# First feed-forward product of a decoder layer: two of eight pairs of k-tiles as seven block products instead of eight

## The chip, the cores and the metric

The kernel runs on one core of a Trainium2 chip. The metric is the device time of one execution in microseconds. Three executions of the kernel before took 1478.36, 1482.99 and 1483.57 us (median 1482.99); the profiled execution took 1481.03 us, of which its trace spans 1478.9 us.

## The reference

One layer of a decoder over 256 tokens of width 2048: a token mixer, a cross attention and a gated feed-forward part, each followed by a residual and a LayerNorm. Only the feed-forward part is touched:

```python
def swiglu(x, w_in, w_out):          # x 256x2048, w_in 2048x11264, w_out 5632x2048
    g, u = jnp.split(x @ w_in, 2, axis=-1)
    return (jax.nn.silu(g) * u) @ w_out
```

The left half of the columns of `x @ w_in` is the gate, the right half the linear part.

## The kernel before

Every float32 product is made of three TensorE passes. `split` (lines 116 to 118) writes a high part (ScalarE, `ACTIVATE`, L117) and a low part (VectorE, source minus high part, `TENSOR_TENSOR`, L118) of an operand; the product is then high x high, high x low, low x high, accumulated in PSUM (L229 to L231 in `chunk_mm`, or L268 to L270 in `mm3`).

The activations x (`x2T`, four `Quad`s of 4 k-tiles x 256 tokens) lie transposed and split in SBUF. The weights are streamed. `chunk_in` (L199) loads a chunk of two k-tiles x 512 columns (512 KB) into one of 5 `raw` buffers and splits it into one of 4 `hl` buffers; `chunk_mm` then runs 6 matmuls for each of the two token tiles, so a chunk is 12 matmuls of 128x512. `product` (L233) does this for 8 chunks.

The first feed-forward product has 11 column groups `j` of 512 columns (here: rounds). A round is a `product` for the gate columns, whose two PSUM tiles go through Silu (L865, ScalarE), and a `product` for the linear columns; VectorE then multiplies the two (L877), and `keep` writes the result h to DRAM (L196, a 256 KB `spill` in two DMAs). To be the stationary operand of the second feed-forward product, h must be transposed: `turned` loads it back from DRAM in another order (four DMAs, L181, tile `turn`), transposes it in blocks on VectorE (four instructions, L187, tile `tr`), and splits it (ScalarE L188, VectorE L190). `turn` is a generator; `flush` advances it by one step after each chunk of the next product: loads after its first chunk, transposes and L188 after the second, L190 after the third.

All loads, spills and turns are issued by SyncE's one queue (SP), in order. A load waits until the chunk five before it has been split (`raw` has 5 buffers); the split of a chunk waits until TensorE has used the chunk four before it (`hl` has 4). The written order is only a start: a scheduler that simulates a timeline reorders the instructions of each engine, and that order is then fixed. [...] The pool `big` holds 14 tiles `b8` of 8 KB per partition, a `Quad` in each.

Of the kernel before, what the change touches and what calls it, by code (L numbers as in the profile page):

```python
# [28 lines left out]
DFF = 5632  # L29
# [36 lines left out]
def trunk(ctx: ExitStack, tc: tile.TileContext, a, out: bass.AP):  # L66
    nc = tc.nc
    const = ctx.enter_context(tc.tile_pool(name="const", bufs=1))
    big = ctx.enter_context(tc.tile_pool(name="big", bufs=14))
    stream = ctx.enter_context(tc.tile_pool(name="stream", bufs=3))  # L70
    work = ctx.enter_context(tc.tile_pool(name="work", bufs=2))
# [60 lines left out]
    for tt in range(NT):  # L132
        k = P * (tt + 1)
# [88 lines left out]
    def chunk_mm(o, act, tt, c, kts, n, w):  # L222
        hi, lo = w
        sl = slice(tt * P, (tt + 1) * P)
        for kk in range(KC):
            k = c * KC + kk
            q = act[k // 4]
            xh, xl = q.hi[:, k % 4, sl], q.lo[:, k % 4, sl]
            nc.tensor.matmul(o[:, :n], xh, hi[:, kk, :n], start=k == 0, stop=False)  # L229
            nc.tensor.matmul(o[:, :n], xh, lo[:, kk, :n], start=False, stop=False)  # L230
            nc.tensor.matmul(o[:, :n], xl, hi[:, kk, :n], start=False, stop=k == kts - 1)  # L231

    def product(act, pieces, steps=1, before=None, first=None, seq=0, stream_seq=0, done=None):  # L233
# [137 lines left out]
    for ps in wide(w_in[:, C_QI:C_KI], load_x):  # L371
        t = b8().rearrange("p (h t) -> p h t", h=8)
        for tt in range(NT):
            sl = slice(tt * P, (tt + 1) * P)
# [3 lines left out]
            for i in range(2):  # L378
                p = ps_aux(F32R)
# [19 lines left out]
    for tt in range(NT):  # L399
        sl = slice(tt * P, (tt + 1) * P)  # L400
        p = ps[tt]
# [6 lines left out]
        st = work.tile([P, 6], F32, tag="st1", name=nm("st1"))  # L408
# [260 lines left out]
    for j in range(4):  # L669
        cs = slice(j * W, (j + 1) * W)  # L670
# [5 lines left out]
    for j in range(4):  # L676
        cs = slice(j * W, (j + 1) * W)
# [3 lines left out]
        for tt in range(NT):  # L681
            g = stage()
# [18 lines left out]
    tok = []  # L701
# [101 lines left out]
    for j in range(4):  # L803
        cs = slice(j * W, (j + 1) * W)
# [28 lines left out]
    ws = {}  # L833
# [21 lines left out]
    x2T = n2.quads  # L855


    hT = []
    wf = a["w_ffn_in"][0]
    for j in range(DFF // W):  # L860
        gs = []

        def gate(tt, p):
            g = stage()
            nc.scalar.activation(g, p, AF.Silu)  # L865
            gs.append(g)

        if j == 0:
# [5 lines left out]
        q = Quad()  # L874
        d = spill()
        for tt in range(NT):
            nc.vector.tensor_tensor(gs[tt], gs[tt], pu[tt], op=ALU.mult)  # L877
            keep(d, tt, gs[tt])
# [36 lines left out]
```

## Time and profile before

| | |
|---|---|
| times of 3 runs | 1478.36, 1482.99, 1483.57 us |
| profiled execution, its span | 1481.03, 1478.9 us |
| TensorE (PE) busy | 1456.7 us, 98% |
| VectorE (DVE) busy | 917.5 us, 62% |
| ScalarE (ACT) busy | 670.8 us, 45% |
| GpSimd (POOL) busy | 19.5 us, 1% |
| DMA queue, share of 16 engines | 69.4% |
| loads of the first feed-forward weights | 176 of 512 KB |

Matmuls are pipelined, so that a record of one is longer than the step to the next, and busy TensorE says only that there was always one under way. The 176 loads are 11 rounds of 16 chunks.

### The profile page before, as it was taken

What the parts mean: (1) busy time and instruction counts of PE and PEld (TensorE: products, weight loads), DVE (VectorE), ACT (ScalarE), POOL (GpSimd) and SP (SyncE); (2) the same over time, 40 slices, a digit from 0 to 9 for tenths busy, and PEclk for the clock granted to TensorE, in tenths of its full rate; (3) what the DMA queues carried; (4) which work ended last, traced back from release to release, by engine and by line L of the source; (5) the groups of instructions that cost most, each with busy time, mean ns of one, the idle gap of its engine ahead of it and who ended that gap; (6) DMA issues with size and microseconds to landing.
All of it is one profiled execution on the core that took longest, in us unless ns stands there. A gap on an engine that the chain in (4) does not pass through costs nothing.

```text
span 1478.9 us, 17743 instructions
## 1 busy us (share of the span) xinstructions
PE 1456.7 (98%) x6656; PEld 1210.6 (82%) x6656; DVE 917.5 (62%) x1151; ACT 670.8 (45%) x778; POOL 19.5 (1%) x43
## 2 busy tenths in 40 slices
PE   8999999999999999999989999999999999999997
PEld 6988888888888888888778888888888888888885
DVE  5575986575856666885875455555545555545446
ACT  4554456454544444545544344444444444343331
POOL 0000000000000000000000000000000000000000
PEclk9999999999999999999999999999999999999998
DMA  9884667777667779968536766676667667666662
GB/s 281 189 272 143 197 216 225 230 237 222 221 191 233 219 259 305 229 191 264 171 129 201 226 215 212 219 223 222 206 207 233 213 216 254 190 197 196 193 220 100
DMA packets 197462, 316.60 MB, mean 214 GB/s; under 512 B 18688, under 2 KB 58752, under 8 KB 197376
## 3 DMA queue, kind: packets, MB, share of 16 engines
q1 hardware_dynamic: 197376, 315.47, 69.4%
q8 instruction: 52, 0.85, 0.3%
q14 instruction: 34, 0.28, 0.1%
HBM read 298.65 MB, written 16.78 MB: 213 GB/s over the span
## 4 chain that ended last, share of the span: by engine, by line
PE 93%; DMA 3%; DVE 2%; issue 1%; POOL 0%; ACT 0%; SPq 0%; POOLq 0%; DVEq 0%; ACTq 0%
PE acc L230 29%; PE acc L231 29%; PE acc L229 29%; DMA raw<-in_w_in 1%; PE aux L269 1%; PE aux L270 1%; PE aux L268 1%; DVE b L751 1%; DMA turn<-spill 1%; DMA kvg<-in_kv_norm_g 1%; PE acc L269 0%; PE acc L270 0%; DVE hl L118 0%; DVE lnst L733 0%; PE acc L268 0%
## 5 line engine op out<-in xcount | busy, mean ns | idle before, releaser
L118 DVE TENSOR_TENSOR hl<-raw,hl 128x1024 fp32r<-128x1024 f32 (+2 forms) x495 | 596.2, 1212 | 432.1 <-ACT hl L117 431.4
L117 ACT ACTIVATE hl<-raw 128x1024 fp32r<-128x1024 f32 (+2 forms) x495 | 517.7, 1052 | 604.5 <-PE acc L231 541.5
L230 PE MATMUL acc<-hl,b 128*128 128x512 f32 (+1 forms) x1912 | 743.1, 389 | 0.3 <-DVE hl L118 0.2
L231 PE MATMUL acc<-hl,b 128*128 128x512 f32 (+1 forms) x1912 | 742.9, 389 | 0.0
L229 PE MATMUL acc<-hl,b 128*128 128x512 f32 (+1 forms) x1912 | 740.9, 389 | 0.7 <-ACT b L117 0.7
L230 PEld LDWEIGHTS acc<-hl,b 128*128 128x128 f32 x1912 | 359.4, 188 | 73.4 <-DVE hl L118 1.1
L229 PEld LDWEIGHTS acc<-hl,b 128*128 128x128 f32 x1912 | 359.4, 188 | 73.2 <-ACT b L117 0.9
L231 PEld LDWEIGHTS acc<-hl,b 128*128 128x128 f32 x1912 | 359.4, 188 | 73.1 <-DVE b L118 0.2
L187 DVE STREAM_TRANSPOSE tr<-turn 128x256 f32<-128x256 f32 (+1 forms) x148 | 67.0, 510 | 82.5 <-DMA turn<-spill 82.5
L188 ACT ACTIVATE b<-tr 128x1024 fp32r<-128x1024 f32 (+1 forms) x37 | 37.4, 1014 | 92.4 <-DVE tr L187 89.1
L190 DVE TENSOR_TENSOR b<-tr,b 128x1024 fp32r<-128x1024 f32 (+1 forms) x37 | 42.8, 1162 | 3.5 <-ACT b L188 3.0
L117 ACT ACTIVATE b<-aux 128x512 fp32r<-128x512 f32 (+1 forms) x48 | 25.6, 542 | 37.3 <-PE aux L161 21.6
L118 DVE TENSOR_TENSOR b<-aux,b 128x512 fp32r<-128x512 f32 (+1 forms) x48 | 28.7, 617 | 3.8 <-ACT b L117 3.6
L230 PE MATMUL acc<-b,b 128*128 128x512 f32 x72 | 28.2, 394 | 1.3 <-DVE b L118 1.3
L229 PE MATMUL acc<-b,b 128*128 128x512 f32 x72 | 28.1, 394 | 0.1
L231 PE MATMUL acc<-b,b 128*128 128x512 f32 x72 | 27.9, 390 | 0.0
L269 PE MATMUL acc<-hl,b 128*128 128x512 f32 x64 | 25.4, 404 | 0.5 <-DVE hl L118 0.4
L270 PE MATMUL acc<-hl,b 128*128 128x512 f32 x64 | 24.6, 394 | 0.0
L118 DVE TENSOR_TENSOR b<-raw,b 128x1024 fp32r<-128x1024 f32 x18 | 21.4, 1218 | 5.0 <-ACT b L117 5.0
L269 PE MATMUL aux<-b,b 128*128 128x256 f32 (+1 forms) x80 | 21.8, 281 | 0.0
L268 PE MATMUL acc<-hl,b 128*128 128x512 f32 x64 | 20.7, 410 | 1.1 <-ACT hl L117 1.1
L865 ACT ACTIVATE stage<-acc 128x512 f32<-128x512 f32 x22 | 13.2, 599 | 18.7 <-PE acc L231 18.7
(123 smaller groups left out, 569.9 us busy)
## 6 DMA issues: line engine op xcount, KB each, us to landing
raw<-in_w_ffn_in SPq DMA_DIRECT2D x176, 512.0 KB, 4.2
raw<-in_w_in SPq DMA_DIRECT2D x143, 512.0 KB, 4.4
raw<-in_w_ffn_out SPq DMA_DIRECT2D x88, 512.0 KB, 4.3
raw<-in_w_out SPq DMA_DIRECT2D x32, 512.0 KB, 8.0
spill<-stage SPq DMA_DIRECT2D x56, 256.0 KB, 4.0
turn<-spill SPq DMA_DIRECT2D x104, 128.0 KB, 3.3
raw<-in_w_o_dsa SPq DMA_DIRECT2D x16, 512.0 KB, 4.7
raw<-in_w_o_moba SPq DMA_DIRECT2D x16, 512.0 KB, 4.4
```

The source lines that it names most:

```text
L117: nc.scalar.activation(hi, src, AF.Copy)
L118: return (eng or nc.vector).tensor_tensor(lo, src, f(hi), op=ALU.subtract)
L187: nc.vector.transpose(tr[:, i, :], v[:, i])
L188: nc.scalar.activation(hi, tr, AF.Copy)
L190: nc.vector.tensor_tensor(lo, tr, f(hi), op=ALU.subtract)
L229: nc.tensor.matmul(o[:, :n], xh, hi[:, kk, :n], start=k == 0, stop=False)
L230: nc.tensor.matmul(o[:, :n], xh, lo[:, kk, :n], start=False, stop=False)
L231: nc.tensor.matmul(o[:, :n], xl, hi[:, kk, :n], start=False, stop=k == kts - 1)
L268: nc.tensor.matmul(o, lh, rh, start=start, stop=False)
L269: nc.tensor.matmul(o, lh, rl, start=False, stop=False)
L270: nc.tensor.matmul(o, ll, rh, start=False, stop=stop)
L751: prev = nc.vector.scalar_tensor_tensor(t, t, scalar, self.rows[row][:, j * W:(j + 1) * W], op0=op0, op1=op1)
```

## The change

Round 0 stays as it was. Rounds 1 to 10 do the gate and the linear columns together. For a pair of k-tiles (chunk `c`), the two token tiles x two k-tiles are a 2x2 block matrix A, and two k-tiles x (gate, linear) are a 2x2 block matrix B; the result is a 2x2 block of PSUM tiles (x11, x12, x21, x22). `plain_cell` makes the eight block products of a chunk as before (two chunks, 24 matmuls). `fast_cell`, for the chunks 0 and 1 only (fast cells A and B here), makes seven products in the Strassen-Winograd form: 21 matmuls. For that it needs

- on the activation side, four sums per chunk, made once in round 0 (`fast_acts`: 8 additions of 128x128, 8 transposes, split into the `Quad` `sq`);
- on the weight side, in every round, four subtractions of 128x512 on VectorE (`tb`, `tcs`) and four splits, of the 1024-wide B11/B12 (`ha`), `tb` (`hb`), `tcs` (`hc`) and of the 512-wide B22;
- on the output side, four more PSUM banks for the products m1, m5, m6, m7, taken from `aux`, and `sums` (one copy, four additions, VectorE), whose results are added to x11 to x22 at the round's end.

The round's end is now six VectorE instructions (L990, L992, L993) in place of two (L877). The chunks run in the order 0, 2, 3, 1, 4, 5, 6, 7.

```diff
+    FAST = (0, 1)
+    ORDER = (0, 2, 3, 1, 4, 5, 6, 7)
...
+    def fast_acts():
+        q = Quad()
+        for t, c in enumerate(FAST):
+            st = stage()
...
+            nc.vector.tensor_tensor(s1, a21, a22, op=ALU.add)
+            nc.vector.tensor_tensor(s2, s1, a11, op=ALU.subtract)
+            nc.vector.tensor_tensor(s3, a11, a21, op=ALU.subtract)
+            nc.vector.tensor_tensor(s4, a12, s2, op=ALU.subtract)
+            to_quad(q, t, st)
+        return q
...
+            self.t[name] = ps_acc() if name[0] == "x" else ps_aux()
...
+    def fast_cell(bk, act, sq, t, c, ws, stop):
...
+        r0, r1 = [load_chunk(w, c) for w in ws]
+        ha, la = hl_tile()
+        lows.append(split(ha, la, r0))
+        hb, lb = hl_tile()
+        tb = work.tile([P, 2, W], F32, tag="tw", name=nm("tw"), bufs=1)
+        nc.vector.tensor_tensor(tb[:, 0], r1[:, 0], r0[:, 0], op=ALU.subtract)
+        nc.vector.tensor_tensor(tb[:, 1], r1[:, 1], r1[:, 0], op=ALU.subtract)
+        hc, lc = hl_tile()
+        tcs = work.tile([P, 2, W], F32, tag="s", name=nm("s"))
+        nc.vector.tensor_tensor(tcs[:, 0], r1[:, 1], tb[:, 0], op=ALU.subtract)
+        nc.vector.tensor_tensor(tcs[:, 1], r0[:, 1], tcs[:, 0], op=ALU.subtract)
+        b22 = work.tile([P, 2, W], F32R, tag="s", name=nm("s"))
+        split(b22[:, 0], b22[:, 1], r1[:, 1])
+        split(hb, lb, tb)
+        lows.append(split(hc, lc, tcs))
+        bk.mm("m1", a11, (ha[:, 0], la[:, 0]), stop)
+        bk.mm("m5", s1, (hb[:, 0], lb[:, 0]), stop)
+        bk.mm("m7", s3, (hb[:, 1], lb[:, 1]), stop)
+        bk.mm("m6", s2, (hc[:, 0], lc[:, 0]), stop)
+        bk.mm("x11", a12, (ha[:, 1], la[:, 1]))
+        bk.mm("x12", s4, (b22[:, 0], b22[:, 1]))
+        bk.mm("x21", a22, (hc[:, 1], lc[:, 1]))
...
+    def plain_cell(bk, act, c, ws, stop):
...
+            for tt in range(NT):
+                for kk in range(KC):
+                    bk.mm(f"x{tt + 1}{n + 1}", act_of(q, k + kk, tt), (hi[:, kk], lo[:, kk]), stop and kk == KC - 1)
+            flush()
...
+    def sums(bk):
+        m = bk.t
+        c11, c12, c21, c22 = [stage() for _ in range(4)]
+        nc.scalar.activation(c11, m["m1"], AF.Copy)
+        nc.vector.tensor_tensor(c12, c11, m["m6"], op=ALU.add)
+        nc.vector.tensor_tensor(c21, c12, m["m7"], op=ALU.add)
+        nc.vector.tensor_tensor(c12, c12, m["m5"], op=ALU.add)
+        nc.vector.tensor_tensor(c22, c21, m["m5"], op=ALU.add)
...
-            product(x2T, [wf[:, j * W:(j + 1) * W]], done=gate)
-        pu = product(x2T, [wf[:, DFF + j * W:DFF + (j + 1) * W]])
...
+            for i, c in enumerate(ORDER):
+                if c in FAST:
+                    fast_cell(bk, x2T, sq, FAST.index(c), c, ws, c == FAST[-1])
+                    flush()
...
+                    if c == FAST[-1]:
+                        cs = sums(bk)
+                else:
+                    plain_cell(bk, x2T, c, ws, i == len(ORDER) - 1)
+            for tt in range(NT):
+                g, u = cs[2 * tt:2 * tt + 2]
+                nc.vector.tensor_tensor(g, g, bk.t[f"x{tt + 1}1"], op=ALU.add)
+                nc.scalar.activation(g, g, AF.Silu)
+                nc.vector.tensor_tensor(u, u, bk.t[f"x{tt + 1}2"], op=ALU.add)
+                nc.vector.tensor_tensor(g, g, u, op=ALU.mult)
+                keep(d, tt, g)
```

The scheduler's order on three places of a middle round. First VectorE, where the transposes of the last round's h stand. Before, just after the multiplication of a round and three splits of the next:

```order
L877 TENSOR_TENSOR stage_1107_7491<-stage_1107_7491,acc_1109_7495 128x512
L877 TENSOR_TENSOR stage_1108_7493<-stage_1108_7493,acc_1110_7496 128x512
L118 TENSOR_TENSOR hl_1140_7706<-raw_1139_7704,hl_1140_7706 128x1024
L118 TENSOR_TENSOR hl_1142_7723<-raw_1141_7721,hl_1142_7723 128x1024
L118 TENSOR_TENSOR hl_1144_7740<-raw_1143_7738,hl_1144_7740 128x1024
L187 STREAM_TRANSPOSE tr_1136_7680<-turn_1133_7658 128x256 x4
L118 TENSOR_TENSOR hl_1146_7757<-raw_1145_7755,hl_1146_7757 128x1024
L190 TENSOR_TENSOR b8_1127_7633<-tr_1136_7680,b8_1127_7633 128x1024
```

Now they stand amid the work for fast cell B (`raw_1106`, `raw_1107` are its two chunks, `tw` is `tb`, `s_1112` `tcs`, `s_1113` B22, and `hl_1108`, `hl_1109`, `hl_1111` are `ha`, `hb`, `hc`):

```order
L915 TENSOR_TENSOR tw_1110_7275<-raw_1107_7269 128x512
L187 STREAM_TRANSPOSE tr_1098_7208<-turn_1095_7186 128x256 x4
L918 TENSOR_TENSOR s_1112_7279<-raw_1107_7269,tw_1110_7275 128x512
L118 TENSOR_TENSOR hl_1108_7271<-raw_1106_7267,hl_1108_7271 128x1024
L118 TENSOR_TENSOR s_1113_7282<-raw_1107_7269,s_1113_7282 128x512
L919 TENSOR_TENSOR s_1112_7279<-raw_1106_7267,s_1112_7279 128x512
L190 TENSOR_TENSOR b8_1022_6803<-tr_1098_7208,b8_1022_6803 128x1024
L118 TENSOR_TENSOR hl_1109_7274<-tw_1110_7275,hl_1109_7274 128x1024
L118 TENSOR_TENSOR hl_1111_7278<-s_1112_7279,hl_1111_7278 128x1024
L118 TENSOR_TENSOR hl_1119_7321<-raw_1118_7319,hl_1119_7321 128x1024
```

Between the transposes and the split of the next plain chunk (`hl_1119`, chunk 4) stand seven instructions, where there was none. In the rounds 8 and 9 L190 is not there: those `Quad`s find no free `b8` until round 10. In round 10 L187 stands behind `hc`.

Second VectorE at the end of a round. Before, the plain splits run up to the multiplication (the rows are of another round, its last three chunks):

```order
L118 TENSOR_TENSOR hl_1174_7941<-raw_1173_7939,hl_1174_7941 128x1024
L118 TENSOR_TENSOR hl_1177_7963<-raw_1176_7961,hl_1177_7963 128x1024
L118 TENSOR_TENSOR hl_1180_7986<-raw_1179_7984,hl_1180_7986 128x1024
L877 TENSOR_TENSOR stage_1149_7789<-stage_1149_7789,acc_1151_7793 128x512
```

Now fast cell A of the next round (chunks `raw_1136`, `raw_1137`) is prepared ahead of the round's end; `hl_1129`, `hl_1131`, `hl_1133` are the plain chunks before it. The load of `raw_1137` waits for the buffer of `raw_1126`, which the split of `hl_1127` frees:

```order
L118 TENSOR_TENSOR hl_1127_7389<-raw_1126_7387,hl_1127_7389 128x1024
L118 TENSOR_TENSOR hl_1129_7406<-raw_1128_7404,hl_1129_7406 128x1024
L914 TENSOR_TENSOR tw_1140_7475<-raw_1137_7469,raw_1136_7467 128x512
L915 TENSOR_TENSOR tw_1140_7475<-raw_1137_7469 128x512
L118 TENSOR_TENSOR hl_1131_7423<-raw_1130_7421,hl_1131_7423 128x1024
L918 TENSOR_TENSOR s_1142_7479<-raw_1137_7469,tw_1140_7475 128x512
L118 TENSOR_TENSOR s_1143_7482<-raw_1137_7469,s_1143_7482 128x512
L919 TENSOR_TENSOR s_1142_7479<-raw_1136_7467,s_1142_7479 128x512
L118 TENSOR_TENSOR hl_1133_7440<-raw_1132_7438,hl_1133_7440 128x1024
```

Two 512-wide subtractions that need both chunks of cell A now stand ahead of the split of `hl_1131`; behind `hl_1133` come `ha`, `hb`, two L990, `hc`, two L992 and two L993.

Third TensorE. Before, a chunk's 12 matmuls stand in written order, high, low, high, as here its first three:

```order
L229 MATMUL acc_1129_7639<-hl_1144_7740,b8_903_6017 128x512
L230 MATMUL acc_1129_7639<-hl_1144_7740,b8_903_6017 128x512
L231 MATMUL acc_1129_7639<-hl_1144_7740,b8_903_6017 128x512
```

In fast cell B the matmuls that need only a high part are drawn ahead; its last ten:

```order
L268 MATMUL aux_1091_7170<-hl_1111_7278,b8_943_6305 128x512
L268 MATMUL acc_1094_7182<-hl_1111_7278,b8_901_6015 128x512
L269 MATMUL aux_1089_7162<-hl_1109_7274,b8_943_6305 128x512
L270 MATMUL aux_1089_7162<-hl_1109_7274,b8_943_6305 128x512
L269 MATMUL aux_1090_7166<-hl_1109_7274,b8_943_6305 128x512
L270 MATMUL aux_1090_7166<-hl_1109_7274,b8_943_6305 128x512
L269 MATMUL aux_1091_7170<-hl_1111_7278,b8_943_6305 128x512
L270 MATMUL aux_1091_7170<-hl_1111_7278,b8_943_6305 128x512
L269 MATMUL acc_1094_7182<-hl_1111_7278,b8_901_6015 128x512
L270 MATMUL acc_1094_7182<-hl_1111_7278,b8_901_6015 128x512
```

The low part of `hc` is first read by the fourth matmul from the cell's end, the eighteenth of 21.

## Rows read from the trace of the kernel before

**Rows 1.** The page: busy time, and the chain that ended last.

```profile
PE 1456.7 (98%) x6656; PEld 1210.6 (82%) x6656; DVE 917.5 (62%) x1151; ACT 670.8 (45%) x778; POOL 19.5 (1%) x43
PE 93%; DMA 3%; DVE 2%; issue 1%; POOL 0%; ACT 0%; SPq 0%; POOLq 0%; DVEq 0%; ACTq 0%
```

**Rows 2.** Windows: us, busy by engine, granted clock, DMA; ten rounds, sum and mean.

```profile
985.00:1028.00 43.00, 43.00 (x192) 35.61 (x191) 22.68 (x23) 18.38 (x20) 0.00 (x0) 1.00 0.68 215
...
sum 435.00, PE 435.00 PEld 360.32 DVE 233.46 ACT 183.67 POOL 0.00; mean PE 43.50 PEld 36.03 DVE 23.35 ACT 18.37 POOL 0.00
```

**Rows 3.** Timeline of PE: start, us; two matmuls twelve apart in one product.

```profile
1000.30 0.39 PE L229 MATMUL acc<-hl,b 128*128 128x512 f32 x1
...
1003.02 0.39 PE L229 MATMUL acc<-hl,b 128*128 128x512 f32 x1
```

**Rows 4.** Timeline of DVE around a round's end; brackets: idle before, and releaser.

```profile
1009.75 1.23 DVE L118 TENSOR_TENSOR hl<-raw,hl 128x1024 fp32r<-128x1024 f32 x1 [1.50 <-ACT hl L117]
1010.89 1.28 DVE L877 TENSOR_TENSOR stage<-stage,acc 128x512 f32<-128x512 f32 x2
...
1022.50 2.17 DVE L187 STREAM_TRANSPOSE tr<-turn 128x256 f32<-128x256 f32 x4 [3.36 <-DMA turn<-spill]
1024.60 1.18 DVE L118 TENSOR_TENSOR hl<-raw,hl 128x1024 fp32r<-128x1024 f32 x1
```

**Rows 5.** Timeline of DVE, an earlier product: a chain of 512-wide instructions.

```profile
452.84 1.28 DVE L693 TENSOR_TENSOR stage<-stage,acc 128x512 f32<-128x512 f32 x2
454.04 1.28 DVE L694 TENSOR_TENSOR stage<-stage,b 128x512 f32<-128x512 f32 x2
455.24 1.22 DVE L118 TENSOR_TENSOR hl<-raw,hl 128x1024 fp32r<-128x1024 f32 x1
```

**Rows 6.** Timeline of SP around the same round's end as in the DVE rows.

```profile
1011.60 0.94 SPq L196 DMA_DIRECT2D spill<-stage  x2
1013.73 0.38 SPq L210 DMA_DIRECT2D raw<-in_w_ffn_in  x1
1016.63 1.80 SPq L181 DMA_DIRECT2D turn<-spill  x4
```

**Rows 7.** Waits, ten rounds: engine line waited for, us in total, times, longest.

```profile
DVE hl L118 <- ACT hl L117: 161.0, 121, 2.0
DVE tr L187 <- DMA turn<-spill: 30.9, 10, 5.0
```

**Rows 8.** Timeline of DVE: the longest and the shortest way from L877 to L187.

```profile
1097.93 1.28 DVE L877 TENSOR_TENSOR stage<-stage,acc 128x512 f32<-128x512 f32 x2
1111.17 2.17 DVE L187 STREAM_TRANSPOSE tr<-turn 128x256 f32<-128x256 f32 x4 [4.99 <-DMA turn<-spill]
...
1141.45 1.28 DVE L877 TENSOR_TENSOR stage<-stage,acc 128x512 f32<-128x512 f32 x2
1151.80 2.20 DVE L187 STREAM_TRANSPOSE tr<-turn 128x256 f32<-128x256 f32 x4 [2.11 <-DMA turn<-spill]
```

**Rows 9.** Tile `raw`, ten rounds: the last line, on its loads.

```profile
DMA to landing us min/median/max: 3.4/4.2/7.4
```

**Rows 10.** Lines: groups of instructions, busy us, mean ns of one, idle before.

```profile
L117 ACT ACTIVATE hl<-raw 128x1024 fp32r<-128x1024 f32 (+2 forms) x495 | 517.7, 1052 | 604.5 <-PE acc L231 541.5 <-DMA raw<-in_w_in 18.5 <-issue 16.6
L230 PEld LDWEIGHTS acc<-hl,b 128*128 128x128 f32 x1912 | 359.4, 188 | 73.4 <-DVE hl L118 1.1
...
L694 DVE TENSOR_TENSOR stage<-stage,b 128x512 f32<-128x512 f32 x8 | 5.1, 683 | 0.0
```

**Rows 11.** Tile `stage`: ns min/median/max, first and last start; eight transposes.

```profile
L161 PE MATMUL aux<-ident,stage x8: 270/272/273, 689.4 to 690.7; 128*128 128x128 f32 x8
```

More of the change, by code (lines that the diff above doesn't have):

```diff
@@ L855, in trunk @@
     x2T = n2.quads
+    FAST = (0, 1)
[4 more added lines that the diff above has]
+            st = stage()
+            a11, a12 = [tok[0][:, (2 * c + i) * P:(2 * c + i + 1) * P] for i in range(2)]
+            a21, a22 = [tok[1][:, (2 * c + i) * P:(2 * c + i + 1) * P] for i in range(2)]
+            s1, s2, s3, s4 = [st[:, i * P:(i + 1) * P] for i in range(4)]
+            nc.vector.tensor_tensor(s1, a21, a22, op=ALU.add)
[4 more added lines that the diff above has]
+        return q
@@ new lines, in trunk, with __init__, mm, load_chunk @@
+    class Banks:
+        def __init__(self, last_cell):
+            self.t, self.begun = {}, set()
+            self.last_cell = last_cell
+        def mm(self, name, x, w, stop=False):
+            if name not in self.t:
+                self.t[name] = ps_acc() if name[0] == "x" else ps_aux()
+            (xh, xl), (wh, wl) = x, w
+            mm3(self.t[name], xh, xl, wh, wl, name not in self.begun, stop)
+            self.begun.add(name)
+    def load_chunk(w, c, mixed=False):
+        raw = stream.tile([P, KC, W], F32, tag="raw", name=nm("raw"), bufs=5)
+        last[0] = nc.sync.dma_start(raw, w[c * KC * P:(c + 1) * KC * P, :].rearrange("(k p) n -> p k n", p=P))
+        return raw
@@ new lines, in hl_tile, with act_of @@
+    def hl_tile():
+        t = stream.tile([P, D], F32R, tag="hl", name=nm("hl"), bufs=4)
+        return [t[:, i * KC * W:(i + 1) * KC * W].rearrange("p (k n) -> p k n", k=KC) for i in range(2)]
+    def act_of(q, k, tt):
+        sl = slice(tt * P, (tt + 1) * P)
+        return q.hi[:, k, sl], q.lo[:, k, sl]
+    def fast_cell(bk, act, sq, t, c, ws, stop):
+        q, k = act[c * KC // 4], c * KC % 4
+        a11, a12, a22 = act_of(q, k, 0), act_of(q, k + 1, 0), act_of(q, k + 1, 1)
+        s1, s2, s3, s4 = [act_of(sq, i, t) for i in range(4)]
+        r0, r1 = [load_chunk(w, c) for w in ws]
[20 more added lines that the diff above has]
+        bk.mm("x21", a22, (hc[:, 1], lc[:, 1]))
@@ new lines, in plain_cell @@
+    def plain_cell(bk, act, c, ws, stop):
+        q, k = act[c * KC // 4], c * KC % 4
+        for n, w in enumerate(ws):
+            raw = load_chunk(w, c)
+            hi, lo = hl_tile()
+            lows.append(split(hi, lo, raw))
+            for tt in range(NT):
+                for kk in range(KC):
+                    bk.mm(f"x{tt + 1}{n + 1}", act_of(q, k + kk, tt), (hi[:, kk], lo[:, kk]), stop and kk == KC - 1)
+            flush()
+            side.step(1)
+    def sums(bk):
[6 more added lines that the diff above has]
+        nc.vector.tensor_tensor(c22, c21, m["m5"], op=ALU.add)
+        return c11, c12, c21, c22
@@ L858, in trunk @@
     hT = []
     wf = a["w_ffn_in"][0]
+    sq = None
     for j in range(DFF // W):
@@ L866, in gate @@
             gs.append(g)
+        q = Quad()
+        d = spill()
         if j == 0:
@@ L870, in trunk @@
             side.finish()
-        else:
-            product(x2T, [wf[:, j * W:(j + 1) * W]], done=gate)
-        pu = product(x2T, [wf[:, DFF + j * W:DFF + (j + 1) * W]])
[L874 to L878, printed above, removed]
+            sq = fast_acts()
+            pu = product(x2T, [wf[:, DFF + j * W:DFF + (j + 1) * W]])
+            for tt in range(NT):
+                nc.vector.tensor_tensor(gs[tt], gs[tt], pu[tt], op=ALU.mult)
+                keep(d, tt, gs[tt])
+        else:
+            ws = [wf[:, j * W:(j + 1) * W], wf[:, DFF + j * W:DFF + (j + 1) * W]]
+            bk = Banks(None)
+            for i, c in enumerate(ORDER):
+                if c in FAST:
+                    fast_cell(bk, x2T, sq, FAST.index(c), c, ws, c == FAST[-1])
+                    flush()
+                    side.step(1)
+                    if c == FAST[-1]:
+                        cs = sums(bk)
+                else:
+                    plain_cell(bk, x2T, c, ws, i == len(ORDER) - 1)
+            for tt in range(NT):
+                g, u = cs[2 * tt:2 * tt + 2]
[4 more added lines that the diff above has]
+                keep(d, tt, g)
         later.append(turn(q, d))
```

## The prediction

> **What bounds the kernel now.** I began with the busy shares and the chain that ended last: TensorE is busy 98% of the span and makes 93% of the chain [rows 1]. [...] Two matmuls twelve apart start 2.72 us apart [rows 3]: a step is 0.2267 us, and a round of 16 chunks is 16 x 2.72 = 43.5 us, as the windows have it. VectorE waits before its splits for ScalarE 121 times, 161 us in all [rows 7], which is harmless: ScalarE waits for TensorE to free a buffer [rows 10]. It also waits for the transposed h to come back from DRAM, ten times, 30.9 us [rows 7]. That wait costs nothing today, since three plain chunks lie split ahead of TensorE. It is the wait on which this change turns.
>
> **TensorE's side.** Each fast cell drops 3 of 24 matmuls, so 6 a round and 60 in ten rounds: 60 x 0.2267 = 13.6 us. An undisturbed round becomes 12 x 2.72 + 42 x 0.2267 = 42.16 us. The eight transposes for `fast_acts` are new: seven steps of such took 1.3 us [rows 11], so eight take 1.5 us, once. If nothing else happened, the change would gain 12.1 us.
>
> **VectorE's side.** Prices of one step in a queue that doesn't wait: a 1024-wide split 1.14 us (1009.75 to 1010.89) [rows 4]; a 512-wide instruction 0.60 us, since two L693 and two L694 take 1.20 us each, though the second pair needs the first's results [rows 5]. The last of a chain counts whole: 1.23 us. The trace has no subtraction of two streamed tiles, but L694 reads and writes SBUF in that form at 0.683 us [rows 10], and L693, which reads PSUM, has 1.28 - 0.60 = 0.68 [rows 5]: where the operands lie makes no difference here. Bounds for its step are 0.60 and the record's 0.68; I take 0.60, as a queue of independent steps is what stands there. Four transposes take 2.10 us until the next starts [rows 4]. A round's busy time grows by two fast cells (each 3 x 1.23 + 5 x 0.68 = 7.1 us), four `sums` (2.7) and four more at the end (2.7), less four plain splits (4.9): 14.7 us, so 23.35 + 14.7 = 38 of some 43 us. On average it still fits; what counts is order.
>
> **Where the stall forms.** The transposes L187 stand in front of most of fast cell B's preparation. I follow the loop from the moment D at which `hc`'s low part in cell B is written to the next such moment.
>
> 1. From D to the first L993. Along TensorE: restart after a wait, which no row shows, 0.25 us by my estimate (a weight load of 0.188 [rows 10] that no matmul covers, and a semaphore; bounds 0 and 0.39, a whole matmul record [rows 3], 2 us of the sum either way); four matmuls, 0.9; chunks 4 to 7, 8 x 2.72 = 21.76; the last result visible and L992, about 0.8. Together 23.7 us. Along VectorE: the splits of chunk 4, chunk 5 and half of chunk 6 with the four `sums` between them take 5 x 1.14 + 4 x 0.60 = 8.1 us, and the last of them frees the buffer for cell A's second weight tile. Its load takes 4.2 us in the median (3.4 to 7.4) [rows 9] and 0.1 to issue, and VectorE waits for it, as the subtractions for A stand ahead of chunk 7. From there come five 512-wide steps (`tb`, `tcs`, B22), four of the round's end (L990, L992) and five splits (chunk 7 twice, `ha`, `hb`, `hc`): 9 x 0.60 + 5 x 1.14 = 11.1 us. Together 23.5 us. The two ways are equal within what I can read; I take 23.7.
> 2. From L993 to the transposes. Spill and reload stand in SP's queue as before, with one weight load between. Before, the first L877 started at 1010.89 and L187 at 1022.50: 11.61 us [rows 4], in which the reload was issued at 1016.63, 5 us after the first spill [rows 6]. VectorE waited 3.36 us there, and 3.09 in the mean of ten [rows 7], so the mean way is 11.61 - 0.27 = 11.3 us; the bounds are 10.35 and 13.24 [rows 8].
> 3. From L187 to the next D: four transposes 2.10, three 512-wide steps 1.80, the splits `ha`, L190 and `hb` 3.42, `hc` 1.23: 8.55 us.
>
> The loop takes 23.7 + 11.3 + 8.55 = 43.6 us, against 42.16 for TensorE alone. So TensorE waits 1.4 us a round in cell B, for `hb`'s and `hc`'s low parts, and the round ends up 0.1 us longer than before. The matmuls saved are given back to a trip through DRAM that used to be hidden.
>
> **The sum.** Seven rounds (1 to 7) go round this loop: 7 x 0.1 = +0.7 us. In rounds 8 and 9 L190 has left the chain (-1.14): 2 x -1.04 = -2.1. In round 10 the transposes stand behind `hc`; it costs 42.16 us, or -1.4. With +1.5 for the activation sums the total is -1.3 us. The profiled execution of 1481.03 us would become 1479.7; the median of the runs lies 2.0 us above it, so I predict 1482 us. The 8 `fast_acts` additions of 128x128 lie on VectorE in round 0, where it idles between splits; without that cover they'd cost 8 x 0.3 us, half the 512-wide step. ScalarE gains six 1024-wide splits, two 512-wide ones and a copy and loses four, 2 x 1.05 + 3 x 0.53 = 3.7 us of the 25 that it idles a round [rows 2, 10]: hidden, though `hc`'s high part follows the second `tcs` step; it is ready 1 us before VectorE gets to it.
>
> With every round at 10.35 us the loop is 42.6 us and TensorE hardly waits in rounds 8 to 10: 7 x -0.9 - 2 x 1.4 - 1.4 + 1.5 = -9 us. At 13.24 it is 45.5: 7 x 2.0 + 2 x 0.9 - 1.4 + 1.5 = +16 us.
>
> [...] VectorE's queue steps overlap in the rows: 0.60 us from start to start for a record of 0.68 [rows 5]. [...]
>
> **Rivals.**
> - *The reload is in time* (0.15). If h comes back under 9.9 us after L993, the wait in cell B is gone: -13.6 + 1.5 = -12.1, 1471 us. For it: the loads have gaps. Against: none of the ten was below 10.35.
> - *The loop is longer* (0.20). Both halves hang on a DMA: from a landing of 4.4 us on, VectorE's way decides step 1, and each us is a us of the loop. At 5.2 us there, and half a us more in the reload, since three weight loads now queue right behind it, a round is 1.3 us longer: 7 x 1.4 + 2 x 0.3 - 1.4 + 1.5 = +10.5 us, 1493. For it: 7.4 as the longest landing [rows 9]. Against: that chunk's load is far from a reload.
> - *VectorE's steps don't overlap* (0.05): if each 1024-wide step took its record of 1.23 us [rows 4] and each 512-wide one its 0.68 [rows 5], 0.08 to 0.09 more a step, VectorE's way to L993 would be 25.2 and the loop 2.1 us longer: 7 x 2.2 + 2 x 1.1 + 0.1 + 1.5 = +19 us, 1502. Against it stand all starts in [rows 4, 5].
> - *Given back in the reload, as summed* (0.60): 1478 to 1489.
>
> **The numbers.** Predicted is the likeliest, 1482 us. A measurement of this kernel tells 0.5%, 7.4 us, from no change. The range, 1470 to 1495, takes in the gain and most of the longer loop. Faster by over 0.5% (under 1475.6) 0.17: the reload in time, and a little of the sum's lower bound; within 0.5% 0.59; slower (over 1490.4) 0.24.
>
> **What would show it.** Windows of a round: 43.3 to 43.9 us with VectorE busy about 38. Waits: TensorE's weight loads or matmuls on VectorE's low parts in cell B, about 1.4 us a round, where none were; L187 waiting for the reload 2 to 4 us; the first subtraction for cell A waiting for a weight load about 3 us. Rounds 8 to 10 visibly shorter. Wrong would be a wait of TensorE elsewhere (the first chunks after cell A, or for a PSUM bank), a reload that takes under 10 us, or step times of VectorE other than 0.60 and 1.14.

## The result and the profile after

The changed kernel takes 1469.86 us (median of five runs, 1467.96 to 1474.44), the kernel before 1480.25 us beside it: a ratio of 0.993, 95% interval 0.9912 to 0.9948. It is faster by 0.7%, where no change was forecast, and lies just below the range of 1470 to 1495. What came true is the rival *the reload is in time*. The profiled execution took 1469.42 us, 11.6 less than that of before (the medians differ by 10.4); the rival's sum was 12.1.

The page, busy time and shares of the chain that ended last (as [rows 1] of before):

```profile
PE 1444.1 (98%) x6604; PEld 1198.4 (82%) x6604; DVE 1045.3 (71%) x1361; ACT 706.8 (48%) x830; POOL 19.6 (1%) x43
PE 91%; DMA 4%; DVE 3%; issue 1%; ACT 0%; POOL 0%; SPq 0%; POOLq 0%; DVEq 0%; ACTq 0%
```

Windows of rounds 2 and 5, from one L993 to the next (columns as in [rows 2]):

```profile
837.18:880.73 43.55, 43.42 (x191) 35.27 (x190) 36.10 (x45) 22.85 (x25) 0.00 (x0) 1.00 0.67 217
964.71:1006.95 42.24, 42.24 (x188) 34.91 (x187) 36.18 (x45) 22.20 (x25) 0.00 (x0) 1.00 0.70 224
```

TensorE has no gap in round 5, which is about as long as its 42.16 us of matmuls. Rounds 4 to 9 take 42.24 us each, round 3 41.74 and round 10 41.86; of the rounds 2 to 10 only round 2, with 43.55, is held up.

Waits from 800 to 1220 us (as [rows 7]):

```profile
DVE tw L914 <- DMA raw<-in_w_ffn_in: 31.1, 13, 4.2
...
DVE tr L187 <- DMA turn<-spill: 14.8, 8, 2.7
...
PEld aux L269 <- DVE hl L118: 1.2, 3, 0.6
```

VectorE waits for weight loads before the fast cells, and for the reload half as long as before. TensorE waits for a low part 1.2 us in all; the prediction had 1.4 in every round.

VectorE from cell A's first subtraction to cell B's last split in one round (as [rows 4, 8]):

```profile
952.99 0.69 DVE L914 TENSOR_TENSOR tw<-raw,raw 128x512 f32<-128x512 f32 x1 [3.04 <-DMA raw<-in_w_ffn_in]
...
964.71 1.29 DVE L993 TENSOR_TENSOR stage<-stage,stage 128x512 f32<-128x512 f32 x2
965.91 3.58 DVE L118 TENSOR_TENSOR hl<-raw,hl 128x1024 fp32r<-128x1024 f32 x3
...
974.37 2.17 DVE L187 STREAM_TRANSPOSE tr<-turn 128x256 f32<-128x256 f32 x4 [2.09 <-DMA turn<-spill]
...
981.64 1.22 DVE L118 TENSOR_TENSOR hl<-s,hl 128x1024 fp32r<-128x1024 f32 x1
```

From L993 to L187 it is 9.66 us here. The eight ways of the rounds 2 to 9 are 10.56, 9.40, 9.33, 9.66, 9.57, 9.37, 9.24 and 9.38, a mean of 9.56; before it was 11.3, and the shortest was 10.32 (880.34 to 890.66; [rows 8] call 10.35 the shortest, which is the second). The one above 9.9 is that of round 2: there the reload is issued 2.7 us after the spill, about as in round 5, but takes 5.3 us to land in the median, against 4.0. From L187 to the end of `hc` it is 981.64 + 1.22 - 974.37 = 8.49 us, where 8.55 was predicted.

SyncE's queue around that round's end, and the DMA issues of the same stretch (KB of one, median us to landing):

```profile
958.39 1.50 SPq L894 DMA_DIRECT2D raw<-in_w_ffn_in  x2
965.42 0.95 SPq L196 DMA_DIRECT2D spill<-stage  x2
967.16 0.38 SPq L894 DMA_DIRECT2D raw<-in_w_ffn_in  x1
968.18 1.80 SPq L181 DMA_DIRECT2D turn<-spill  x4
```

```profile
spill<-stage SPq DMA_DIRECT2D x20, 256.0 KB, 2.1
```

So a spill is two DMAs of 256 KB each, 512 KB a round, and not 256 KB in all. The same two views of the kernel before, at the end of the round of [rows 4, 6]:

```profile
1011.00 0.37 SPq L210 DMA_DIRECT2D raw<-in_w_ffn_in  x1
```

```profile
spill<-stage SPq DMA_DIRECT2D x18, 256.0 KB, 4.4
```

The DMA engines in the change as the spill is issued (window, columns as in [rows 2]; the last two are DMA share and GB/s):

```profile
965.00:966.00 1.00, 1.00 (x6) 0.82 (x5) 1.00 (x3) 0.06 (x1) 0.00 (x0) 1.00 0.00 0
```

Here is the difference. Before, a weight load of 512 KB was issued at 1011.00, 0.6 us ahead of the spill at 1011.60: the plain split of 1009.75 [rows 4] had just freed its buffer. The spill was issued while that load was in flight, and its median landing was 4.4 us. Now no load is issued from 959.9 (958.39 + 1.50) to 967.16. VectorE spends that time on `hb`, `hc` and the round's end, which free no `raw` buffer; the next is freed by the first split behind L993, which ends at 967.13 (965.91 + 1.22). So the spill finds the DMA engines idle and lands in 2.1 us. I call this gap in the loads the lull; that it is the cause is tested in experiments 5 and 6.

### The profile page after: what moved, and what is told of

Its sections match the earlier page's. It is cut to its first block, busy times and chain, and to the rows that moved or that the text cites. A ratio compares the mean times of both kernels' runs of the same rounds, so it can differ in the third digit from the quotient of the medians.

```text
span 1467.3 us, 17933 instructions
## 1 busy us (share of the span) xinstructions
PE 1444.1 (98%) x6604; PEld 1198.4 (82%) x6604; DVE 1045.3 (71%) x1361; ACT 706.8 (48%) x830; POOL 19.6 (1%) x43
## 4 chain that ended last, share of the span: by engine, by line
PE 91%; DMA 4%; DVE 3%; issue 1%; ACT 0%; POOL 0%; SPq 0%; POOLq 0%; DVEq 0%; ACTq 0%
PE acc L230 20%; PE acc L231 20%; PE acc L229 19%; PE acc L270 8%; PE acc L269 8%; PE acc L268 8%; PE aux L269 2%; PE aux L270 2%; PE aux L268 2%; DMA turn<-spill 1%; DMA raw<-in_w_in 1%; DVE b L751 1%; DVE hl L118 1%; DMA kvg<-in_kv_norm_g 1%; DMA spill<-stage 0%
## 5 line engine op out<-in xcount | busy, mean ns | idle before, releaser
L118 DVE TENSOR_TENSOR hl<-raw,hl 128x1024 fp32r<-128x1024 f32 (+2 forms) x475 | 571.1, 1212 | 272.3 <-ACT hl L117 271.3
L117 ACT ACTIVATE hl<-raw 128x1024 fp32r<-128x1024 f32 (+2 forms) x475 | 496.3, 1052 | 513.0 <-PE acc L231 347.2
L230 PE MATMUL acc<-hl,b 128*128 128x512 f32 (+1 forms) x1272 | 493.8, 388 | 0.7 <-DVE hl L118 0.5
L231 PE MATMUL acc<-hl,b 128*128 128x512 f32 (+1 forms) x1272 | 493.3, 388 | 0.0
L229 PE MATMUL acc<-hl,b 128*128 128x512 f32 (+1 forms) x1272 | 491.3, 389 | 0.7 <-ACT b L117 0.7
L230 PEld LDWEIGHTS acc<-hl,b 128*128 128x128 f32 x1272 | 238.9, 188 | 48.6 <-DVE hl L118 1.5
L229 PEld LDWEIGHTS acc<-hl,b 128*128 128x128 f32 x1272 | 238.8, 188 | 48.4 <-ACT b L117 0.9
L231 PEld LDWEIGHTS acc<-hl,b 128*128 128x128 f32 x1272 | 238.9, 188 | 48.1 <-DVE b L118 0.2
L269 PE MATMUL acc<-hl,b 128*128 128x512 f32 x584 | 227.8, 391 | 0.5 <-DVE hl L118 0.4
L270 PE MATMUL acc<-hl,b 128*128 128x512 f32 x584 | 226.9, 390 | 0.0
L268 PE MATMUL acc<-hl,b 128*128 128x512 f32 x584 | 210.3, 391 | 0.3 <-ACT hl L117 0.2
L269 PEld LDWEIGHTS acc<-hl,b 128*128 128x128 f32 x584 | 109.9, 188 | 25.1 <-DVE hl L118 2.2
L268 PEld LDWEIGHTS acc<-hl,b 128*128 128x128 f32 x584 | 110.0, 189 | 24.2 <-ACT hl L117 1.1
L270 PEld LDWEIGHTS acc<-hl,b 128*128 128x128 f32 x584 | 109.7, 188 | 22.7
L187 DVE STREAM_TRANSPOSE tr<-turn 128x256 f32<-128x256 f32 (+1 forms) x148 | 67.1, 511 | 64.2 <-DMA turn<-spill 64.1
L190 DVE TENSOR_TENSOR b<-tr,b 128x1024 fp32r<-128x1024 f32 (+1 forms) x37 | 42.8, 1162 | 1.8 <-ACT b L188 1.4
L117 ACT ACTIVATE hl<-s 128x1024 fp32r<-128x1024 f32 x20 | 21.3, 1063 | 31.0 <-DVE s L919 13.3
L914 DVE TENSOR_TENSOR tw<-raw,raw 128x512 f32<-128x512 f32 x20 | 13.8, 691 | 31.2 <-DMA raw<-in_w_ffn_in 31.1
L269 PE MATMUL aux<-hl,b 128*128 128x512 f32 x80 | 31.5, 394 | 0.1
```

Source lines behind the costliest of these rows:

```text
L187: nc.vector.transpose(tr[:, i, :], v[:, i])
L190: nc.vector.tensor_tensor(lo, tr, f(hi), op=ALU.subtract)
```

## The experiments

"Way" is the time from a round's last multiplication (L993 of the change; L990, L1004, L1006, L1009 or L1013 in rows of other kernels) to the transposes (L187, there also L189, L190 or L191); "round" is that from one such multiplication to the next.

**1. A load in flight again.** The dummy load's data is not used; 1-element copies make its two halves wait for the round's end.

```diff
+                if tt == 0:
+                    for k in range(KC):
+                        nc.vector.tensor_copy(dum[k][:, :1], u[:, :1])
+                        nc.sync.dma_start(dum[k], wf[k * P:(k + 1) * P, :W])
                 nc.vector.tensor_tensor(g, g, u, op=ALU.mult)
```

Besides, the rest of cell B's preparation was made to stay behind the transposes.

> One more 512 KB weight load (two of 256 KB, into unused tiles, behind two tiny VectorE copies) is issued just ahead of each round's spill, so that the spill meets a load under way, as it did before the change; the transposes stay ahead of cell B's other preparation. My theory: the change gains because the spill now lands in 2.1 us instead of 4.4, its way to the transposes is 9.4 us and stays under the 9.9 at which TensorE starts to wait. Here the spill lands in 4 us or more, the way from the first last multiplication to the transposes is 11 to 12.5 us, and each of the rounds 1 to 7 is longer by what the way exceeds 9.9: 1.3 to 2.5 us, rounds of 43.5 to 44.7 us; in all 10 to 18 us slower than the change, 1480 to 1488 us, ratio to before 0.999 to 1.006. Rival: the way through DRAM has slack, and the change gains because VectorE is quicker or the wait lies elsewhere: rounds stay at 42.2 us and the time at 1467 to 1473.

Measured: 1520.93 us, ratio 1.0282 (1.0264 to 1.03). Two rows of VectorE and a row of SyncE in one round:

```profile
980.92 1.28 DVE L1004 TENSOR_TENSOR stage<-stage,stage 128x512 f32<-128x512 f32 x2
...
995.14 2.17 DVE L189 STREAM_TRANSPOSE tr<-turn 128x256 f32<-128x256 f32 x4 [4.39 <-DMA turn<-spill]
```

```profile
983.37 1.52 SPq L896 DMA_DIRECT2D raw<-in_w_ffn_in  x2
```

The way is 14.2 us, the round 46.8 to 48.6. The direction is the theory's, the size is not: the scheduler had also moved a second weight load between spill and reload (the row of SyncE has two; the change has one), and VectorE's order in cell B was not quite that of the change. Experiments 5 and 6 take both faults away.

**2 and 3. The same load, with the transposes called two cells later; and that alone.**

```diff
-            flush()
+            if c not in (2, 3):
+                flush()
```

> The same extra load in flight, but the transposes of the last round's h stand behind the splits of cell B (the generator is not advanced after the chunks 2 and 3). My theory: with the same long way nothing waits for it, since the next thing behind the transposes is the split of a plain chunk that TensorE needs later: 1466 to 1473 us, ratio 0.990 to 0.995. Rival (the extra traffic itself costs, by making weight loads late): as slow as the run with the load and the early transposes, 1480 or more.

> The change with only the transposes moved behind the splits of cell B. My theory: the wait there is nearly gone already, what is left is round 2 (1.3 us) and some tenths, so 1 to 3 us faster than the change: 1466 to 1470 us, ratio 0.990 to 0.993. Rival (TensorE still loses more than a tenth of a us a round to that chain): 4 us or more faster than the change, under 1466.

Measured: 1472.01 us (0.9944, 0.9928 to 0.9959) with the load, 1471.18 (0.9935, 0.9923 to 0.9948) without. The transposes now stand behind cell B's splits in VectorE's own order, 15.0 to 16.3 us after the multiplication with the load and 14.5 to 14.8 without, and in neither does VectorE wait for the reload in the rounds 2 to 9. A row of the run with the load, with no wait in brackets:

```profile
1028.92 2.17 DVE L187 STREAM_TRANSPOSE tr<-turn 128x256 f32<-128x256 f32 x4
```

With it 49 us of experiment 1's loss are gone. So it is not the loads as such that cost most of that time, but the reload's place in VectorE's queue. Wholly free the load is not: the profiled execution, at 1476.70 us the slowest of six, has rounds of 41.1 to 44.2 us, and VectorE waits 59.0 us for weight loads before the fast cells, against 31.1 in the change. Without the load the late call takes the hold out of round 2, which is 42.24 us, but the times show no gain on the change: the 1 to 3 us that I had expected do not appear.

**4. Pairs of columns with no fast cell;** the round's end is one Silu and one multiplication again (L990 there).

```diff
-    FAST = (0, 1)
-    ORDER = (0, 2, 3, 1, 4, 5, 6, 7)
+    FAST = ()
+    ORDER = (0, 1, 2, 3, 4, 5, 6, 7)
```

> Rounds 1 to 10 by column pairs as in the change, but every cell plain: eight block products each, no sums, no four extra banks. My theory: the gain is that of the 60 matmuls alone, so this one is as slow as before: 1477 to 1484 us, ratio 0.998 to 1.002, rounds of 43.5 us. Rival (working by pairs, with the weight loads in another rhythm, gains something by itself): under 1476, ratio below 0.997.

Measured: 1484.89 us, ratio 1.003 (1.0019 to 1.004). SyncE's queue at a round's end:

```profile
875.66 0.37 SPq L894 DMA_DIRECT2D raw<-in_w_ffn_in  x1
878.18 0.34 SPq L196 DMA_DIRECT2D spill<-stage  x1
879.32 0.37 SPq L894 DMA_DIRECT2D raw<-in_w_ffn_in  x1
879.91 0.34 SPq L196 DMA_DIRECT2D spill<-stage  x1
881.10 0.37 SPq L894 DMA_DIRECT2D raw<-in_w_ffn_in  x1
884.34 1.81 SPq L181 DMA_DIRECT2D turn<-spill  x4
```

```profile
PEld acc L269 <- DVE hl L118: 5.2, 7, 1.7
```

Plain splits free a buffer every 2.7 us, so loads stand before, between and behind the two spills: the way of this round is 12.6 us (877.47 to 890.07), 12.2 in the mean of the rounds 2 to 9. VectorE waits 58.3 us for the reload in ten rounds, and TensorE 5.2 us for low parts that are split behind it. The whole is 5.0 us slower than before, 0.9 us beyond what I had expected. The pairs by themselves gain nothing; the fast cells, 15 us faster than this, carry the whole gain and bring the lull with them.

**5 and 6. The disputed size by itself.** In the rounds before the last, VectorE's order in cell B is made binding as the change has it, each step behind the one before. The control has no load. The other has experiment 1's, 512 KB, and to keep SyncE's order that of the control:

```diff
-        last[0] = nc.sync.dma_start(raw, w[c * KC * P:(c + 1) * KC * P, :].rearrange("(k p) n -> p k n", p=P))
+        with tc.issue_after(back[0].ins) if c == 4 and back[0] is not None else nullcontext():
+            last[0] = nc.sync.dma_start(raw, w[c * KC * P:(c + 1) * KC * P, :].rearrange("(k p) n -> p k n", p=P))
```

where `back` is the last DMA of the reload.

> Control: VectorE's order of the change in cell B made binding, with no extra load. It should be the change again: rounds of 42.24 us, way from L993 to the transposes 9.2 to 10 us, 1467 to 1473 us.

> As the control, with 512 KB more loaded just ahead of the spill in SyncE's queue; again one weight load stands between spill and reload, and VectorE's order is that of the control. Theory, the way lasts as long as the DMA engines need for what is moved in it (some 2.1 MB in the change, 2.5 to 2.6 MB before, at 190 to 250 GB/s): 0.5 MB more, of which some falls into the idle stretch, makes it 10.5 to 12 us. From about 10 us on TensorE waits, so a round takes 42.5 to 44.2 us and the whole 1473 to 1487 us. Rival, the way was short for another reason (nothing waited for at its start, the queue's order): 9.2 to 10 us as in the control, 1467 to 1473 us.

Measured: 1470.40 us (0.9928, 0.9911 to 0.9946) for the control, 1477.41 (0.9976, 0.9966 to 0.9985) with the load. In the control the ways have a mean of 9.46 us, and the rounds 6 to 9 are 42.23 to 42.24 us each. One of its ways, 9.49 us, and a row of its waits:

```profile
1136.19 1.29 DVE L1006 TENSOR_TENSOR stage<-stage,stage 128x512 f32<-128x512 f32 x2
...
1145.68 2.21 DVE L190 STREAM_TRANSPOSE tr<-turn 128x256 f32<-128x256 f32 x4 [1.72 <-DMA turn<-spill]
```

```profile
PEld aux L272 <- DVE hl L118: 1.4, 3, 0.8
```

With the load, SyncE, VectorE and the same row of the waits:

```profile
970.30 0.82 SPq L1012 DMA_DIRECT2D dum<-in_w_ffn_in  x2
971.16 0.91 SPq L200 DMA_DIRECT2D spill<-stage  x2
972.70 0.38 SPq L899 DMA_DIRECT2D raw<-in_w_ffn_in  x1
975.33 1.80 SPq L185 DMA_DIRECT2D turn<-spill  x4
```

```profile
970.25 1.28 DVE L1013 TENSOR_TENSOR stage<-stage,stage 128x512 f32<-128x512 f32 x2
...
981.32 2.16 DVE L191 STREAM_TRANSPOSE tr<-turn 128x256 f32<-128x256 f32 x4 [1.66 <-DMA turn<-spill]
...
1013.95 1.28 DVE L1013 TENSOR_TENSOR stage<-stage,stage 128x512 f32<-128x512 f32 x2
```

```profile
PEld aux L273 <- DVE hl L118: 8.6, 16, 0.8
```

The spill waits for the load as before the change: 4.2 us from its issue to that of the reload, which waits for it (2.8 in the change). The way is 11.07 us here and 10.98 in the mean of eight. The rest of the loop is 1013.95 - 981.32 = 32.6 us in this round, 32.5 in the mean of the rounds 2 to 7 (31.8 in the rounds 8 and 9, which lack L190); the prediction's steps 1 and 3 had 23.7 + 8.55 = 32.25. The round is 43.3 us in the mean of eight, and TensorE waits for low parts in cell B, as the prediction described. This is the predicted kernel, without the lull. A rival would be that the added bytes delay the weight loads and so lengthen the rest of the loop. The control speaks against it: its two long ways, 10.92 and 10.03 us, have rounds of 43.24 and 42.47 us, a rest of 32.3 and 32.4 with no load added.

**7. Half that load,** 256 KB, in the same order, bound in round 10 too (`for k in range(1)` in experiment 1's loop).

> One extra load of 256 KB stands ahead of the spill in SyncE's queue (before: two of 256 KB and another order of VectorE in cell B; here VectorE keeps the order of the change, made binding). If the way from L993 to the transposes is short only because no weight load is under way at the spill, the spill lands in 3 to 5 us, the way is 10 to 12.5 us and the round is the way plus 33.0 us: 43 to 45.5 us, 1476 to 1490 us in all, with TensorE waiting in cell B. Rival, the way is short for another reason (the order of the queue, the time of its issue): the way stays at 9.2 to 9.9 us, the round at 42.24, and the time at 1467 to 1473 us.

Measured: 1478.41 us (0.9974, 0.9961 to 0.9987). The time falls in the theory's interval, but not by its mechanism: the ways stay at 9.1 to 9.95 us, and the rounds at 42.24 but for 42.34 in round 2, as the rival had it. One of the ways, 9.28 us:

```profile
1007.37 1.28 DVE L1009 TENSOR_TENSOR stage<-stage,stage 128x512 f32<-128x512 f32 x2
...
1016.65 2.17 DVE L189 STREAM_TRANSPOSE tr<-turn 128x256 f32<-128x256 f32 x4 [1.56 <-DMA turn<-spill]
```

The spill lands later (3.1 us) and the reload correspondingly sooner (3.1 for 4.0). Probably these 256 KB fall into DMA time that was idle: over the ways of the rounds 5 and 6, 9.77 and 9.28 us, the DMA share is 0.84 and 0.80, over the change's, 9.66 and 9.57 us, 0.76 and 0.72. No run shows at what size between 256 and 512 KB the way begins to grow. The 8 us come from round 10, which takes 49.9 us instead of 41.9: there the bound order keeps cell B behind transposes that wait for the split of an earlier `Quad`, which gets its buffer only then. The row of that wait, and windows of the stop, TensorE's granted clock third from the end:

```profile
DVE b L192 <- ACT b L190: 6.7, 1, 6.7
```

```profile
1195.00:1197.00 2.00, 0.00 (x0) 0.00 (x0) 2.00 (x4) 0.00 (x0) 0.00 (x0) 0.80 0.00 0
1197.00:1200.00 3.00, 2.54 (x6) 2.01 (x7) 2.95 (x5) 1.30 (x2) 0.00 (x0) 0.50 0.29 68
1200.00:1203.00 3.00, 3.00 (x8) 2.33 (x8) 2.80 (x3) 2.13 (x3) 0.00 (x0) 0.50 0.76 287
1203.00:1206.00 3.00, 3.00 (x14) 2.46 (x14) 3.00 (x4) 2.97 (x4) 0.00 (x0) 0.99 0.71 218
```

TensorE stands idle from 1193.3 to 1197.5, a wait of 4.1 us for a low part, and then works at a granted clock of 0.50 for some 6 us: eight matmul records in 3 us where fourteen follow, steps of 0.43 us where 0.23 follows.

**8. One fast cell,** A (`FAST = (0,)`), chunks in natural order.

> Only cell A takes seven products, the chunks run in their natural order. Saved: 30 matmuls x 0.2267 = 6.8 us, less 0.75 us for the four sums' transposes. Theory, pairs of columns alone lose by VectorE's bunched splits behind the reload, and a fast cell gains its matmuls only where the reload is hidden: here the transposes stand amid plain splits and the next weight loads are under way at the spill or not as VectorE lets them, so the time lies between that of the pairs without fast cells less 6 us and that of the change plus 6.8: 1474 to 1480 us. Rival, a fast cell's gain is independent of what stands around the reload: all the change's gain is 60 matmuls, half of it stays, and pairs cost nothing: 1473 to 1476 us with rounds of 42.9 us and no wait of TensorE.

Measured: 1474.46 us (0.9946, 0.9926 to 0.9966), rounds of 42.88 us, TensorE without a gap. 42.88 is about what the matmuls take (14 x 2.72 + 21 x 0.2267 = 42.84): a round saves 0.64 us, half of what it saves in the change, and the whole run 7.4 us, against 10.4 (medians, each beside the kernel before). The transposes stand amid plain splits, so their wait is covered: two ways of 11.00 and 10.65 us leave their rounds at 42.88 and 42.89. It speaks for the rival more than for the middle of my interval: where the reload is covered, each dropped matmul counts.

**9 and 10. A third cell,** chunk 4, with the transposes called two cells later as in experiment 3; and the same with all cells' subtractions on GpSimd (L914, L915, L918, L919).

```diff
-    FAST = (0, 1)
-    ORDER = (0, 2, 3, 1, 4, 5, 6, 7)
+    FAST = (0, 1, 4)
+    ORDER = (0, 2, 3, 1, 5, 4, 6, 7)
...
-        nc.vector.tensor_tensor(tb[:, 0], r1[:, 0], r0[:, 0], op=ALU.subtract)
+        nc.gpsimd.tensor_tensor(tb[:, 0], r1[:, 0], r0[:, 0], op=ALU.subtract)
```

> A third cell (chunk 4) takes seven products, the chunks run 0, 2, 3, 1, 5, 4, 6, 7, the transposes are called for two cells later. TensorE's own time is 41.5 us a round, 6.8 us less than the change over ten rounds, plus 0.75 us for sums. VectorE is busy 36.2 us of a round in the change and gets 4.1 more: 40.3 of 41.5. Theory, VectorE waits for loads and for the reload at least 3 us a round, so it becomes the bound: rounds of 43 us or more, TensorE waiting for low parts, 1470 to 1485 us. Rival, order is all that counts and 40.3 us fit: 1462 to 1465 us.

> The three cells again, with the four subtractions of each cell on GpSimd in place of VectorE. VectorE is busy some 33 us of a round. If GpSimd makes one 128x512 subtraction in under about 1.5 us, the preparation is in time and the round is TensorE's 41.5 us: 1462 to 1466 us, faster than the change. If it takes 2 us or more, or slows VectorE down while both read SBUF, cell B waits for it and the time is 1475 us or more.

Measured: 1481.69 us (0.9997, 0.9982 to 1.0012) and 1494.09 (1.0081, 1.006 to 1.0101). A round of the first, by windows:

```profile
924.99:968.34 43.35, 42.83 (x184) 33.96 (x183) 40.07 (x51) 23.65 (x27) 0.00 (x0) 1.00 0.68 219
```

VectorE is busy 40.07 of 43.35 us, and TensorE has gaps; probably VectorE at this load keeps no reserve for its waits, as I had expected. On GpSimd, a line of the subtractions, lines of the splits beside them, and a window of 200 us:

```profile
L918 POOL TENSOR_TENSOR s<-raw,tw 128x512 f32<-128x512 f32 x29 | 64.0, 2206 | 0.0
```

```profile
L118 DVE TENSOR_TENSOR hl<-raw,hl 128x1024 fp32r<-128x1024 f32 x122 | 181.9, 1516 | 3.2 <-ACT hl L117 3.0
L118 DVE TENSOR_TENSOR hl<-tw,hl 128x1024 fp32r<-128x1024 f32 x28 | 49.0, 1749 | 1.8 <-ACT hl L117 1.3
```

```profile
900.00:1100.00 200.00, 189.39 (x816) 153.04 (x815) 178.97 (x167) 106.05 (x117) 101.28 (x55) 0.99 0.67 210
```

A subtraction takes 1.3 us at the least and 2.2 in the mean of L918, and VectorE's splits, 1.22 us in the change, take 1.52 and 1.75 in the mean. VectorE is busy 178.97 of 200 us, some 40 us in a round of 44.7, as much as with its own subtractions: what it is spared comes back in its other work. Why the two slow down beside each other no run shows.

**11 and 12. Six `raw` buffers,** with two cells and with three.

```diff
-        raw = stream.tile([P, KC, W], F32, tag="raw", name=nm("raw"), bufs=5)
+        raw = stream.tile([P, KC, W], F32, tag="raw", name=nm("raw"), bufs=6)
```

> The change with six raw buffers in place of five (the bias tile has one buffer in place of three, to make room). Two more weight loads stand ahead of the spill in SyncE's queue in every round, so loads should be under way when it starts: by the theory the way from L993 to the transposes grows from 9.5 to 11 to 13 us. But the order of VectorE moves too: the first subtractions of cell B and two of its splits come ahead of the transposes, and only hb, the activation split and hc stand behind them, 2.9 us less. So the stall starts at a way of some 13 us only: rounds of 42.2 us, 1466 to 1474 us. Rival, a buffer more lets all run ahead and the way stays under 10 us.

> Three cells with six raw buffers. VectorE is busy 40.1 us of a round and TensorE 41.5. If the 3 us that VectorE stood in each 43.3 us round with five buffers were waits for loads, they shrink, the round is 41.7 to 42.2 us and the whole 1463 to 1470 us, the first to beat the change. If they come from the chains within a cell (a subtraction, ScalarE's high part, the low part), nothing changes: 1475 to 1483 us.

Measured: 1501.81 us (1.0142, 1.0128 to 1.0155) and 1514.73 (1.0229, 1.0216 to 1.0242). Both times were missed. In the first the way behaves as the theory says: SyncE's and VectorE's rows of one round

```profile
981.86 0.37 SPq L894 DMA_DIRECT2D raw<-in_w_ffn_in  x1
982.46 0.95 SPq L196 DMA_DIRECT2D spill<-stage  x2
```

```profile
1023.23 0.69 DVE L914 TENSOR_TENSOR tw<-raw,raw 128x512 f32<-128x512 f32 x1 [3.37 <-DMA raw<-in_w_ffn_in]
...
1024.44 0.68 DVE L990 TENSOR_TENSOR stage<-stage,acc 128x512 f32<-128x512 f32 x1
```

show a load 0.6 us ahead of the spill, and the eight ways have a mean of 11.27 us, against 9.56 with five buffers. What I had missed is the stretch before L993: with the sixth buffer the scheduler puts cell B's first subtractions ahead of the round's end, where their load isn't there yet. VectorE stands 3.4 us before the second L990, the whole round's end comes later, and the round takes 46.4 us. To make room, the bias tile of earlier stages has one buffer in place of three; this is not where the time goes, since the rounds 1 to 10 alone take 456.1 us (793.47 to 1249.61), against 424.0 in the change. In the second, rounds are of about the same length, and VectorE's waits for weight loads before the fast cells are 56.8 us, where experiment 9 has 11.2: they grew instead of shrinking. In both, which of the waits, or the third cell's work, makes up how much of the round was not taken apart.

## Why the prediction was wrong

- **TensorE's side** was right: 42.16 us for an undisturbed round against 42.24, 12.1 us to be had against 11.6 in the profiled execution.
- **VectorE's side** was right: steps of 0.60 and 1.14 us, 36.2 us busy a round (38 predicted), the wait before cell A 3.04 us in the round shown (about 3).
- **Step 3, from L187 to D,** was right: 8.55 predicted, 8.49 measured. **Step 1, from D to L993,** too: 23.7 predicted; with experiment 6's 32.5, less 8.5, it is 24.0 where the loop binds.
- **Step 2, from L993 to the transposes, failed.** It took 11.3 us over from before, on the ground that "spill and reload stand in SP's queue as before, with one weight load between". What stands between them is the same; what stands ahead is not. The load that used to be issued 0.6 us ahead of the spill is now issued behind it, and the way is 9.56 us. My own description of VectorE's order had `hb`, `hc` and the round's end in a row there, none of which frees a `raw` buffer, and I did not ask what this does to SyncE. Experiment 6 puts 512 KB back and finds 10.98 us, rounds of 43.3 and 7.0 us more than its control; experiment 4, without the lull, has 12.2.
- **The threshold,** 9.9 us, was right to 0.2 us: 42.24 - 32.5 = 9.7. In the rounds 3 to 7 the change's ways, 9.33 to 9.66 us, lie 0.1 to 0.4 us below it. The two sides of the forecast were that close together, and the odds given to the rival rested on ten ways measured under other traffic. The rival named the outcome and, with "the loads have gaps", a part of the cause; it did not say why a gap would fall on the spill.
- **VectorE's steps don't overlap**, the rival with the smallest chance, is refuted by 974.37 to 981.64: the transposes and six steps behind them take 7.27 us, 2.10 + 3 x 0.60 + 3 x 1.14 = 7.32 with overlap, and some 0.5 more without. The rival's way to L993, 25.2 us, is 1.7 above the 23.5 of step 1, which is 19 steps at 0.09 us where step 1 lists 23, so the loop would have been a few tenths of a us a round longer still. *The loop is longer* did not occur.

## What to carry to other kernels

Here a round trip's time belonged to the traffic around it, not to the transfer alone: the same 256 KB spill landed in 4.4 us in the median before and in 2.1 after, and the way took 11.3 us and 9.56. So before taking such a time over from the old trace, look for what will be in flight at its start, which here was set by when VectorE frees load buffers. More buffers can lose, when the new order puts an instruction that waits ahead of ones that others wait for (experiment 11: 1501.81 us against 1469.86); more of the cheaper arithmetic can, when the engine that prepares it has hardly any time left (experiment 9: VectorE busy 40.07 of 43.35 us, 1481.69 us in all). And where two ways of a loop come out within a microsecond of each other, the small term that decides deserves the effort.

## What the runs showed that I had not expected

The median landing of a 256 KB spill is 2.1 us with no load under way, 3.1 with 256 KB ahead of it, 3.6 with 512 KB ahead and 4.4 before the change. One buffer more made the same kernel 32 us slower (1501.81 against 1469.86, each beside the same kernel before within 0.6 us). In experiment 7 TensorE ran at a granted clock of 0.50 for some 6 us after a stop that ended at 1197.5 us; with steps of 0.43 us in place of 0.23 that is an estimated 3 us on top of the stop itself.
